# Half of the weights' low parts in a float32 block: a GpSimd subtraction or a transfer that adds

## The chip, the cores and the metric

The kernel runs on one core of a Trainium2 chip, as one launch. The metric is the device time of one execution in microseconds; the figure for a kernel is the median of several executions. Inputs and outputs lie in HBM.

## The reference, cut to what matters

One layer of a hybrid encoder block for 512 tokens and 1024 channels: a shared norm and input projection, an RWKV-7 branch (8 heads of 64) and a chunked Gated DeltaNet branch (4 heads of 128, chunks of 64), a gated merge, an output projection, then an MLP with a causal convolution.

```python
u = rms_norm(x, norm1_g[l])
p = u @ w_in[l]
p_rwkv, qkv, z, a_raw, b_raw, gate_a, gate_b = _split(p, IN_SPLITS)
y_a = rwkv7_mix(p_rwkv, ...) @ rwkv_proj[l]
y_b = gated_deltanet_mix(qkv, z, a_raw, b_raw, ...) @ gdn_proj[l]
mixed = jax.nn.sigmoid(gate_a) * y_a + jax.nn.sigmoid(gate_b) * y_b
x = x + mixed @ w_out[l]
h = causal_depthwise_conv(rms_norm(x, norm2_g[l]) @ ffn_up[l], ffn_conv_w[l])
h_gate, h_up = _split(h, (FFN_HIDDEN, FFN_HIDDEN))
x = x + (jax.nn.silu(h_gate) * h_up) @ ffn_down[l]
```

All of it is float32.

## The kernel before, in words

**Engines.** TensorE (PE) does the matmuls, VectorE (DVE), ScalarE (ACT) and GpSimd (POOL) the rest; SyncE (SP) issues every transfer. Each engine works through its own queue in order.

**Dense products.** A float32 weight is used as a sum of two parts of a format that PE takes at full rate: `hi`, the weight rounded to that format, and `lo`, what is left. An activation is likewise kept as `uh` and `ul`. A product of 128 output channels and 512 tokens is then three kinds of matmul over eight blocks of 128 input channels: lo·uh, hi·uh and hi·ul, 24 in all. `unit` (line 164 on) loads one such weight tile of 128x1024 (512 KB) into `raw` by one transfer on SP, and `halves_of` (line 153) makes `hi` and `lo` for each of its two halves of 128x512: ACT copies to `hi` (line 158), and a subtraction raw − hi gives `lo` (line 160). The subtraction goes by turns to GpSimd (the first half of a unit) and to VectorE (the second half): `POOL = "13"` and the running count modulo 4. `mm3` (line 185 issues its matmuls) uses the first half's `lo` in its first matmul. There are two `raw` buffers and four each of `hi` and `lo` (`HB = 4`), so half n+4 can be written only when PE is through with half n; buffers rotate in the order in which the units are called for.

**Stages.** `first_tiles` (to about 37 us) loads the activations and makes the first units. `mixing` then runs a list of steps, `ORDER`: `R` prepares a pair of RWKV heads (three units), `G` a DeltaNet head (three units), `g` a gate and `z` a DeltaNet gate (one unit each); `i` and `c` are the triangular inverses and the chunk recurrence of RWKV, `I` and `C` those of the DeltaNet heads. After `mixing` come the two branch projections, the merge, and the MLP.

**What sets the order.** The program is written step by step, and a scheduler lays the instructions of all steps into the engines' queues by its own estimates and by priorities: `unit` raises the priority of the load and of the halves, the chunk recurrences run beside the units of later steps. So while DVE works through an inverse, units of the next heads pass through ACT, GpSimd and PE.

**Lines that are spoken of.** `base_inverse` (lines 549 to 571) inverts 32x32 triangles on DVE alone: per row one multiplication into `invN` (line 565) and one addition into `invY` (line 567), each with two inputs in SBUF, one waiting for the other. `rwkv_prep` has DVE operations with two SBUF inputs at lines 496, 510, 512 and 515, `gdn_chain` at line 937; `split` makes `uh` and `ul` at lines 203 and 204. On GpSimd there are also a few small operations: the MEMSETs of lines 557, 641 and 642, the copies of lines 559, 807 and 818, a power of 128x4 elements at line 798.

Of the kernel before, what the change touches and what calls it, by code (L numbers as in the profile page):

```python
# [9 lines left out]
F32 = mybir.dt.float32  # L10
F32R = mybir.dt.float32r
BF16 = mybir.dt.bfloat16
AF = mybir.ActivationFunctionType
ALU = mybir.AluOpType
# [6 lines left out]
POOL = "13"  # L21
# [2 lines left out]
TAGS = {"T": 4, "P": 3, "T2": 2}  # L24
BANKS = {"D": 2, "A": 3, "B": 3}
ORDER = "R0 g0 R1 g1 g2 g3 a i0 G0 G1 z1 c0 z0 g4 g5 R2 I0 R3 C0 g6 i1 c1 g7 g8 G2 G3 g9 z3 g10 z2 g11 I1 g12 C1 g13"
RAWG = 1

BLK = 4
# [67 lines left out]
class Body:  # L97
    def __init__(self, tc, a, o, ctx):
        self.tc, self.nc, self.a, self.o, self.ctx = tc, tc.nc, a, o, ctx
        self.uid = 0  # L100
        self.halves = 0
        self.second = False
        self.spilled = {}

# [46 lines left out]
        self.second = False  # L151


    def halves_of(self, raw, o, w=512):
        nc = self.nc
        hi = self.stream.tile([128, 512], F32R, tag="hi", name=self.nm("hi"), bufs=HB)
        lo = self.stream.tile([128, 512], F32R, tag="lo", name=self.nm("lo"), bufs=HB)
        nc.scalar.activation(hi[:, 0:w], raw[:, o:o + w], AF.Copy)  # L158
        self.halves += 1
        self.on(str(self.halves % 4)).tensor_tensor(out=lo[:, 0:w], in0=raw[:, o:o + w], in1=hi[:, 0:w].bitcast(F32),  # L160
                                                    op=ALU.subtract)
        return hi, lo, w // 128

    def unit(self, src, n=1024, ahead=True):
        nc = self.nc
        parts = []
        with self.tc.high_priority() if ahead else nullcontext():
            raw = self.stream.tile([128, 1024], F32, tag="raw", name=self.nm("raw"), bufs=2)
            nc.sync.dma_start(out=raw[:, 0:n], in_=src)
            for o in range(0, n, 512):  # L170
                parts.append(self.halves_of(raw, o, min(512, n - o)))
        return parts


# [87 lines left out]
    def first_tiles(self, xp):  # L262
# [68 lines left out]
        for i, (m, out) in enumerate(((4, first[1]), (0, first[2]), (8, first[0][:, 8, :]))):  # L331
            self.shifted(m, out, self.dense_in(m, act, "A", after if m == 4 else None), r)
            for k in UN[i]:
# [3 lines left out]
                self.split(self.uh[:, k, :], self.ul[:, k, :], un)  # L337
        for i in range(RAWG):
            self.gate(i, act=act, rstd=r)
# [38 lines left out]
    def mixing(self, first):  # L378
        nc = self.nc
        self.wc = self.mp.tile([128, 4, 8], F32, name="wc")  # L380
        self.rs2 = self.mp.tile([128, 4, 8], F32, name="rs2")
        R, G = {}, {}
        first = {0: first}

        def chain(g):
            self.rwkv_chain(g, R)
            self.rwkv_out((2 * g, 2 * g + 1), R)

        def inverse(g):
            self.gdn_inverse(g, G)  # L390

        for step in ORDER.split():
            op, i = step[0], int(step[1:] or 0)
            if op == "g" and i in self.spilled:
                continue
            if op == "R":
                R[i] = self.rwkv_prep(i, first.get(i))
            elif op == "a":
                self.gdn_gates()
            elif op == "G":  # L400
                G[i] = self.gdn_prep(i)
            elif op == "z":
                self.gdn_z(i)
            elif op == "g":
                self.gate(i)
            else:
                with self.stream2():
                    dict(i=lambda g: self.rwkv_inverse(g, R), c=chain, I=inverse, C=lambda g: self.gdn_chain(g, G))[op](i)
        self.gates = [self.rp.tile([128, 9, T], F32, tag="R", name=self.nm("R")) for _ in range(2)]
        for i in range(16):  # L410
            if i in self.spilled:
                nc.sync.dma_start(out=self.gates[i % 2][:, i // 2, :], in_=self.spilled[i])
            else:
                self.gate(i, self.gates[i % 2][:, i // 2, :])


        y = [self.inv(x) for x in "NAY"]
        y = [t[:, o:o + T] for t in y[:2] for o in (0, T)] + [y[2], self.t("P")] + [self.work.tile([128, T], F32, tag="BK", name=self.nm("BK"), bufs=2) for _ in range(2)]
        y = [t.bitcast(F32R) for t in y]
        for i in range(4):  # L420
            self.split(y[i], y[4 + i], self.yf[:, i, :])
        self.project(0, lambda k: (y[k], y[4 + k]))
# [836 lines left out]
```

## Time and profile before

| | |
|---|---|
| runs | 890.07, 891.26, 891.31 us (median 891.26) |
| the profiled execution | 889.34 us, of which the span of its instructions is 887.6 us |
| busy in the span: PE, DVE, ACT, POOL | 854.3, 653.5, 466.0, 210.3 us (96, 74, 53, 24%) |
| the chain that ended last, by engine | PE 68%, DVE 16%, ACT 6%, issue 3%, POOL under 1% |
| line 160 on POOL | 124 recorded, 170.6 us, 1376 ns each |
| line 160 on DVE | 124, 88.2 us, 711 ns each |
| line 158 on ACT | 248, 152.7 us, 619 ns each |
| TensorE clock granted | 0.997 of full speed |
| transfers | 84.25 MB, 29.6% of the time of the 16 DMA engines |

The busy time of an engine says how long it was at work, not whether anybody waited for it; a matmul's end is modelled and PE's instructions overlap, so PE is busy in the record also while it is not streaming. The chain is followed back from the last instruction: at each step to what released it, or to the instruction before it on its engine. It is the view that says where time would be saved, stage by stage, and it changes as soon as one of its links does.

### The profile page before, as it was taken

The page shows a single profiled execution, that of the slowest core. Times are in us where ns is not written, and L with a number is a line of the kernel's source. Part 1 is how long each engine was busy: PE and PEld are TensorE (multiplying, and loading weights), DVE is VectorE, ACT ScalarE, POOL GpSimd, SP SyncE. Part 2 cuts the span into 40 slices and gives each one's busy share as a digit, 9 for nine tenths or more (in the row PEclk, how much of TensorE's full clock was granted, in tenths as well). Part 3 has the DMA queues.
Part 4 walks back from the last instruction along what each step waited for, and adds up shares of the span by engine and source line. Part 5 has one row for each costly group of instructions (what it writes and reads, how often), then busy time and mean ns, then how long its engine had stood idle before and what let it go on. Part 6 is the DMA issues. An engine that isn't in the chain of part 4 may idle for free.

```text
span 887.6 us, 13504 instructions
## 1 busy us (share of the span) xinstructions
PE 854.3 (96%) x5046; PEld 679.3 (77%) x5046; DVE 653.5 (74%) x1247; ACT 466.0 (53%) x905; POOL 210.3 (24%) x189
## 2 busy tenths in 40 slices
PE   8989999999999899999999999999999999999996
PEld 4867677766777677668788878888888888898895
DVE  6899897973899978944577448998866666573665
ACT  7745357666543677573544455554444444443333
POOL 2231123111111221111122212223222222342431
PEclk9999999999999999999999999999999999999998
DMA  7321222212112211136153223332323332332333
GB/s 265 115 89 59 73 71 73 69 57 68 48 60 72 71 50 60 60 109 213 49 194 113 95 72 95 96 95 98 116 95 95 95 96 89 111 104 82 104 87 132
DMA packets 29746, 84.25 MB, mean 95 GB/s; under 512 B 3312, under 2 KB 5488, under 8 KB 29680
## 3 DMA queue, kind: packets, MB, share of 16 engines
q1 hardware_dynamic: 29680, 83.39, 29.6%
q8 instruction: 40, 0.66, 0.3%
q14 instruction: 26, 0.21, 0.1%
HBM read 77.61 MB, written 5.77 MB: 94 GB/s over the span
## 4 chain that ended last, share of the span: by engine, by line
PE 68%; DVE 16%; ACT 6%; issue 3%; POOL 0%; DVEq 0%; ACTq 0%; POOLq 0%
PE D L185 43%; PE D L1089 5%; PE A L1089 4%; PE B L1089 3%; PE B L185 2%; DVE invN L565 2%; PE A L185 2%; DVE invY L567 2%; DVE P L771 1%; DVE lo L160 1%; DVE R L531 1%; DVE BK L510 1%; DVE BK L515 1%; ACT hi L158 1%; PE B L663 1%
## 5 line engine op out<-in xcount | busy, mean ns | idle before, releaser
L160 POOL TENSOR_TENSOR lo<-raw,hi 128x512 fp32r<-128x512 f32 x124 | 170.6, 1376 | 578.4 <-ACT hi L158 577.2
L158 ACT ACTIVATE hi<-raw 128x512 fp32r<-128x512 f32 x248 | 152.7, 619 | 181.4 <-PE D L185 87.2
L185 PE MATMUL D<-uh,lo 128*128 128x512 f32 x384 | 160.5, 418 | 2.7 <-DVE R L375 1.4
L185 PE MATMUL D<-uh,hi 128*128 128x512 f32 x384 | 151.4, 395 | 0.0
L185 PE MATMUL D<-u2h,lo 128*128 128x512 f32 x352 | 137.9, 392 | 0.0
L185 PE MATMUL D<-u2h,hi 128*128 128x512 f32 x352 | 137.8, 392 | 0.0
L160 DVE TENSOR_TENSOR lo<-raw,hi 128x512 fp32r<-128x512 f32 x124 | 88.2, 711 | 46.3 <-ACT hi L158 45.7
L185 PE MATMUL D<-ul,hi 128*128 128x512 f32 x384 | 109.1, 406 | 0.0
L185 PE MATMUL D<-u2l,hi 128*128 128x512 f32 x352 | 95.1, 392 | 0.0
L185 PEld LDWEIGHTS D<-uh,lo 128*128 128x128 f32 x384 | 72.2, 188 | 21.3 <-issue 3.1
L1006 DVE SCALAR_TENSOR_TENSOR P<-T,vecs,P 128x511 f32<-128x511 f32 x88 | 81.8, 929 | 6.9 <-ACT P L1004 2.6
L185 PEld LDWEIGHTS D<-uh,hi 128*128 128x128 f32 x384 | 72.3, 188 | 14.6 <-issue 1.0
L185 PEld LDWEIGHTS D<-ul,hi 128*128 128x128 f32 x384 | 69.3, 188 | 16.3 <-issue 1.0
L185 PEld LDWEIGHTS D<-u2h,hi 128*128 128x128 f32 x352 | 66.1, 188 | 14.9 <-issue 0.2
L185 PEld LDWEIGHTS D<-u2h,lo 128*128 128x128 f32 x352 | 66.1, 188 | 14.7 <-issue 0.2
L185 PEld LDWEIGHTS D<-u2l,hi 128*128 128x128 f32 x352 | 66.1, 188 | 14.1
L1003 DVE TENSOR_TENSOR T<-D,acc 128x512 f32<-128x512 f32 x44 | 30.2, 686 | 32.0 <-PE D L185 28.2
L565 DVE TENSOR_TENSOR invN<-invA,invY 128x60 f32<-128x60 f32 (+24 forms) x124 | 39.6, 319 | 3.0
L1004 ACT ACTIVATE P<-T,vecs 128x512 f32<-128x512 f32 x44 | 31.7, 721 | 16.5 <-DVE T L1003 14.5
L567 DVE TENSOR_TENSOR invY<-invY,invN 128x60 f32<-128x60 f32 (+24 forms) x124 | 32.3, 260 | 3.0
L771 DVE SCALAR_TENSOR_TENSOR P<-D,vecs,P 128x511 f32<-128x511 f32 (+2 forms) x36 | 26.7, 742 | 0.8 <-ACT P L769 0.7
L1195 ACT ACTIVATE P<-P 128x512 f32<-128x512 f32 x22 | 13.7, 624 | 21.0 <-DVE P L1006 21.0
(437 smaller groups left out, 1556.5 us busy)
## 6 DMA issues: line engine op xcount, KB each, us to landing
raw<-w_in SPq DMA_DIRECT2D x44, 512.0 KB, 3.6
raw<-ffn_up SPq DMA_DIRECT2D x44, 512.0 KB, 3.5
raw<-ffn_down SPq DMA_DIRECT2D x9, 512.0 KB, 3.5
raw<-w_out SPq DMA_DIRECT2D x8, 512.0 KB, 3.5
raw<-ffn_down SPq DMA_DIRECT2D x16, 256.0 KB, 2.9
spill<-T SPq DMA_DIRECT2D x14, 256.0 KB, 2.0
R<-spill SPq DMA_DIRECT2D x14, 256.0 KB, 3.9
raw<-ffn_down SPq DMA_DIRECT2D x9, 384.0 KB, 3.1
```

The costliest lines, as they stand in the source:

```text
L158: nc.scalar.activation(hi[:, 0:w], raw[:, o:o + w], AF.Copy)
L160: self.on(str(self.halves % 4)).tensor_tensor(out=lo[:, 0:w], in0=raw[:, o:o + w], in1=hi[:, 0:w].bitcast(F32), op=ALU.subtract)
L185: nc.tensor.matmul(ps, t[:, w[k]], x[k][p], start=(first and i == 0 and q == 0), stop=(last and i == len(parts) - 1 and q == len(seq) - 1))
L510: nc.vector.scalar_tensor_tensor(out=bkh[h][s, :, sb, :], in0=q(K, s, h), scalar=self.hkk[s, hp:hp + 1], in1=q(at, s, h), op0=ALU.mult, op ...
L565: nc.vector.tensor_tensor(out=w, in0=rows[:, t, 0:t].unsqueeze(2).broadcast_to([128, t, n]), in1=Ym[:, t, c:G].unsqueeze(1).broadcast_to([ ...
L567: nc.vector.tensor_tensor(out=Ym[:, 0:t, c:G], in0=Ym[:, 0:t, c:G], in1=w, op=ALU.add)
L771: nc.vector.scalar_tensor_tensor(out=cv[:, sh:], in0=ps[:, 0:T - sh], scalar=w(3 - sh), in1=cv[:, sh:], op0=ALU.mult, op1=ALU.add)
L1003: nc.vector.tensor_tensor(out=h, in0=ps, in1=self.acc2, op=ALU.mult)
L1004: nc.scalar.activation(cv, h, AF.Copy, scale=w(2))
L1006: nc.vector.scalar_tensor_tensor(out=cv[:, sh:], in0=h[:, 0:T - sh], scalar=w(2 - sh), in1=cv[:, sh:], op0=ALU.mult, op1=ALU.add)
L1089: nc.tensor.matmul(out, w, x, start=bank not in started, stop=stop)
L1195: nc.scalar.activation(g, g, AF.Silu)
```

## The change

`halves_of` gets the source of the load as an argument. In the steps of `ORDER` up to `G3` (the fourth DeltaNet head), where GpSimd would subtract, ACT instead writes −hi into `lo` (line 165 of the changed kernel), and GpSimd issues a transfer that reads the same 256 KB of the weight from HBM once more and adds them onto `lo` in SBUF (line 166). These are 31 halves: R1, g1, g2, g3, G0, G1, z1, z0, g4, g5, R2, R3, g6, g7, g8, G2 and G3. `first_tiles`, the steps after `G3` (g9 to g13, z3, z2), the projections and the MLP keep the subtraction, and so do all halves of VectorE.

```diff
+ACCLAST = "G3"
...
-    def halves_of(self, raw, o, w=512):
+    def halves_of(self, raw, o, w=512, src=None):
         nc = self.nc
         hi = self.stream.tile([128, 512], F32R, tag="hi", name=self.nm("hi"), bufs=HB)
         lo = self.stream.tile([128, 512], F32R, tag="lo", name=self.nm("lo"), bufs=HB)
         nc.scalar.activation(hi[:, 0:w], raw[:, o:o + w], AF.Copy)
         self.halves += 1
+        if src is not None and self.accumulate and str(self.halves % 4) in POOL:
+            nc.scalar.activation(lo[:, 0:w], hi[:, 0:w].bitcast(F32), AF.Copy, scale=-1.0)
+            nc.gpsimd.dma_start(out=lo[:, 0:w], in_=src[:, o:o + w], accum_op=ALU.add)
+            return hi, lo, w // 128
         self.on(str(self.halves % 4)).tensor_tensor(out=lo[:, 0:w], in0=raw[:, o:o + w], in1=hi[:, 0:w].bitcast(F32),
                                                     op=ALU.subtract)
         return hi, lo, w // 128
...
-                parts.append(self.halves_of(raw, o, min(512, n - o)))
+                parts.append(self.halves_of(raw, o, min(512, n - o), src))
...
-        for step in ORDER.split():
+        for n, step in enumerate(ORDER.split()):
             op, i = step[0], int(step[1:] or 0)
+            self.accumulate = n <= ORDER.split().index(ACCLAST)
```

The scheduler lays the queues out anew. Lines of the changed kernel are 8 or 9 higher than before (160 is 168, 158 is 162, 185 is 193, 905 is 914).

ScalarE in G0, the first DeltaNet head: `hi` and `lo` are the halves of its units, `T` and `P` the convolution's tiles. Before:

```order
L158 ACTIVATE hi_1304<-raw_1302 128x512
L774 ACT_TABLE_LOAD
L774 ACTIVATE T_1149<-P_1144 128x512
L769 ACTIVATE P_1188<-D_1163,vecs 128x512
L158 ACTIVATE hi_1308<-raw_1302 128x512
```

The same place in the changed kernel:

```order
L162 ACTIVATE hi_1313<-raw_1311 128x512
L165 ACTIVATE lo_1314<-hi_1313 128x512
L783 ACT_TABLE_LOAD
L783 ACTIVATE T_1156<-P_1151 128x512
L778 ACTIVATE P_1196<-D_1171,vecs 128x512
L162 ACTIVATE hi_1318<-raw_1311 128x512
```

The negative copy stands behind its `hi`, ahead of the work of the head.

GpSimd a little later, in G0 and G1 (`kn` is the key norm, `gs` the gates). Before:

```order
L807 COPY T_1256<-gs 128x512
L160 TENSOR_TENSOR lo_1409<-raw_1406,hi_1408 128x512
L798 TENSOR_TENSOR kn_1196<-kn_1196,mhalf 128x4
L818 COPY gegl<-T_1269 128x4
L160 TENSOR_TENSOR lo_1497<-raw_1494,hi_1496 128x512
```

In the changed kernel:

```order
L816 COPY T_1265<-gs 128x512
L807 TENSOR_TENSOR kn_1204<-kn_1204,mhalf 128x4
L166 DMA lo_1420<-w_in 128x512
L827 COPY gegl<-T_1278 128x4
L166 DMA lo_1509<-w_in 128x512
```

Each subtraction has become the issue of a transfer in the same place; once, as here, it has changed places with a small operation.

TensorE where the recurrence of the first two DeltaNet heads (`B`) begins between the halves of R3 (`D`). Before:

```order
L905 MATMUL B_2597<-G_1108 128x128
L185 MATMUL D_2699<-uh,lo_2692 128x512
L185 MATMUL D_2699<-uh,hi_2691 128x512
L185 MATMUL D_2699<-uh,lo_2692 128x512
L185 MATMUL D_2699<-uh,hi_2691 128x512
L909 MATMUL B_2597<-vn_2599,G_1108 128x128
L912 MATMUL B_2595<-G_1108,vn_2599 128x128
L185 MATMUL D_2699<-uh,lo_2692 128x512
```

In the changed kernel:

```order
L914 MATMUL B_2619<-G_1114 128x128
L193 MATMUL D_2722<-uh,lo_2714 128x512
L193 MATMUL D_2722<-uh,hi_2713 128x512
L193 MATMUL D_2722<-uh,lo_2714 128x512
L193 MATMUL D_2722<-uh,hi_2713 128x512
L193 MATMUL D_2722<-uh,lo_2714 128x512
L193 MATMUL D_2722<-uh,hi_2713 128x512
L193 MATMUL D_2722<-uh,lo_2714 128x512
L193 MATMUL D_2722<-uh,hi_2713 128x512
L193 MATMUL D_2722<-ul,hi_2713 128x512 x4
L918 MATMUL B_2619<-vn_2621,G_1114 128x128
L921 MATMUL B_2617<-G_1114,vn_2621 128x128
```

The recurrence steps move behind the dense work by up to one half (12 matmuls) here; further on other steps move ahead of it by as much. From the projections on, PE's order is the same.

## Rows read from the trace of the kernel before

**Rows 1.** Busy time of each engine in three stretches (us from the start).

```profile
core 0: us, PE busy (x) PEld busy (x) DVE busy (x) ACT busy (x) POOL busy (x), PEclk, DMA share, GB/s
37.00:350.00 313.00, 295.47 (x2126) 223.07 (x2126) 263.94 (x626) 184.92 (x418) 61.60 (x75) 1.00 0.21 69
...
250.00:300.00 50.00, 47.10 (x249) 36.09 (x248) 47.24 (x112) 22.02 (x37) 7.31 (x6) 1.00 0.22 69
...
425.00:888.00 463.00, 453.27 (x2178) 378.17 (x2176) 317.08 (x447) 211.65 (x352) 128.00 (x92) 0.99 0.33 101
```

**Rows 2.** The chain of waits, 37 to 350 us: shares by line.

```profile
by line: PE D L185 18.9%; issue 6.4%; DVE invN L565 6.0%; DVE invY L567 5.2%; DVE P L771 3.3%; DVE lo L160 2.8%; DVE R L531 2.5%; DVE BK L510 2.1%; DVE BK L515 2.0%; ACT hi L158 1.7%; DVE R L496 1.3%; DVE P L512 1.2%; PE B L663 1.2%; ACT R 
```

**Rows 3.** Timeline around 102 us: start, length, instruction, idle time before it.

```profile
102.25 0.22 DVE L567 TENSOR_TENSOR invY<-invY,invN 128x58 f32<-128x58 f32 x1
102.48 1.29 POOL L160 TENSOR_TENSOR lo<-raw,hi 128x512 fp32r<-128x512 f32 x1 [8.43 <-ACT hi L158]
102.50 1.34 DVE L565 TENSOR_TENSOR invN<-invA,invY 128x56 f32<-128x56 f32 x1
```

**Rows 4.** Pieces of the chain of waits in order of time: start, length, what.

```profile
63.96 1.72 DVE P L512
85.08 1.43 DVE BK L510
102.50 1.35 DVE invN L565
...
253.12 1.70 DVE R L496
262.23 1.39 DVE BK L515
...
292.18 1.28 DVE invY L567
...
301.38 1.27 POOL lo L160
```

**Rows 5.** Lines of DVE, 37 to 350 us: count, shortest/median/longest in ns.

```profile
L565 DVE TENSOR_TENSOR invN<-invA,invY x93: 161/241/1342, 101.1 to 315.5; 128x126 f32<-128x126 f32 x6, 128x30 f32<-128x30 f32 x5, 128x56 f32<-128x56 f32 x4, 128x78 f32<-128x78 f32 x4
...
L512 DVE TENSOR_TENSOR P<-P,T x4: 679/688/1706, 64.0 to 261.1; 128x512 f32<-128x512 f32 x4
...
L510 DVE SCALAR_TENSOR_TENSOR BK<-P,sp,T x16: 468/484/1428, 61.9 to 260.3; 64x256 f32<-64x256 f32 x16
...
L496 DVE TENSOR_TENSOR R<-P,Ep x8: 673/682/1776, 56.9 to 255.5; 64x512 f32<-64x512 f32 x8
...
L515 DVE TENSOR_TENSOR BK<-P,T x16: 409/420/1376, 65.7 to 264.1; 64x256 f32<-64x256 f32 x16
...
L160 DVE TENSOR_TENSOR lo<-raw,hi x35: 670/681/1187, 38.6 to 345.1; 128x512 fp32r<-128x512 f32 x35
```

**Rows 6.** Timeline around 47 us: GpSimd writes, DVE works beside it.

```profile
46.63 0.53 POOL L557 MEMSET invY<- 128x512 f32 x1 [1.23 <-DVE T L335]
47.09 0.68 DVE L160 TENSOR_TENSOR lo<-raw,hi 128x512 fp32r<-128x512 f32 x1
47.10 0.20 POOL L641 MEMSET SUV<- 64x128 f32 x1
```

**Rows 7.** Groups by line and form, 37 to 350 us: busy, mean ns, idle before.

```profile
L158 ACT ACTIVATE hi<-raw 128x512 fp32r<-128x512 f32 x69 | 43.2, 626 | 26.8 <-issue 10.9 <-PE D L185 9.3 <-POOL kn L798 4.7
...
L160 POOL TENSOR_TENSOR lo<-raw,hi 128x512 fp32r<-128x512 f32 x34 | 46.6, 1372 | 178.3 <-ACT hi L158 178.3
```

**Rows 8.** Timeline at the first unit of R1.

```profile
37.93 0.64 ACT L158 ACTIVATE hi<-raw 128x512 fp32r<-128x512 f32 x1 [0.49 <-DMA raw<-w_in]
...
44.56 0.40 PE L185 MATMUL D<-uh,lo 128*128 128x512 f32 x1
...
44.80 0.39 PE L185 MATMUL D<-uh,hi 128*128 128x512 f32 x1
```

**Rows 9.** Issues of transfers, whole span: KB each, median us from issue to landing.

```profile
raw<-ffn_down SPq DMA_DIRECT2D x16, 256.0 KB, 2.9
...
raw<-w_in SPq DMA_DIRECT2D x4, 256.0 KB, 5.6
```

More of the change, by code (lines that the diff above doesn't have):

```diff
@@ L101, in __init__ @@
         self.halves = 0
+        self.accumulate = False
         self.second = False
```

## The prediction

> **What bounds the kernel now.** I read the busy times by stretch first. After 425 us PE is at work for 98% of the time, and the change touches nothing there; from 37 to 350 us, the steps in which the 31 halves lie, DVE is busy for 264 of 313 us, in one stretch for 47.2 of 50 [rows 1]. The chain of waits over the same 313 us says who is waited for: PE's dense matmuls hold 18.9% of it, but two lines of the inverse, 565 and 567, hold 11.2% together, and seven more DVE lines are named [rows 2]. So this part is a chain through DVE, with dense matmuls as filling; what DVE saves on the chain ends the stage earlier, and what follows moves with it.
>
> Then the timeline. At 102.48 us GpSimd begins a subtraction of 1.29 us. At 102.50 DVE begins one of its small multiplications and needs 1.34 us for it, until the subtraction ends; the instruction before it, of nearly the same size, took 0.22 [rows 3]. Both read two operands from SBUF. The lines of DVE show the pattern: medians of 0.24 to 0.69 us, the longest ones about 1 us above them [rows 5]. GpSimd is off the chain, yet it stops the engine that is on it.
>
> **What the change removes.** 31 of GpSimd's subtractions, 1.37 us each [rows 7], 42.5 us of an idle engine and worth nothing by themselves. What counts is the stalls of DVE on the chain. I count the pieces of the chain that coincide with one of the 31 subtractions. Eight are of the inverse, from 1.35 us at 102.50 to 1.28 at 292.18 [rows 4], together 9.5 us; eight ordinary ones would be 8 x 0.24 = 1.9 [rows 5], so 7.6 us go. Four are of the head preparation: 1.72 − 0.69 at 63.96, 1.43 − 0.48 at 85.08, 1.70 − 0.68 at 253.12, 1.39 − 0.42 at 262.23 [rows 4, 5], together 4.0 us. One piece is a subtraction itself, 1.27 us at 301.38, where the chain runs through GpSimd and DVE at once [rows 4]. Sum: 7.6 + 4.0 + 1.3 = **12.9 us**, at 13 places of 31.
>
> Not all of that comes back. Behind a DVE instruction that is freed of 1 us stands the next wait, most often for PE (busy 295 of 313 us by the record, if not always streaming [rows 1]) or for ACT. I take eight tenths, 10.3 us: the pieces lie mostly in stretches such as 250 to 300 us, where DVE has next to no idle time, and there a saving is a saving of throughput. The ends are 0 and 12.9 us. Beyond that, the other 18 subtractions may have stalled DVE off the chain; were six of them worth as much as the one at 102.50, 1.1 us, that would be 6.6 us more.
>
> **What it adds on ACT.** 31 copies from SBUF to SBUF of the form of line 158: 31 x 0.626 = 19.4 us [rows 7]. ACT is busy for 185 of 313 us [rows 1], so there is room, but its queue is in order. Of the copies that are there now, 43.2 us [rows 7], 1.7% of 313 = 5.3 us are on the chain [rows 2], 12%. I take the same share of the new ones: **2.4 us** lost. The ends: nothing (all in idle time), and 19.4 us (all on the chain).
>
> **What it adds on GpSimd and in the transfers.** No transfer issued by GpSimd, and none that adds, is in this trace. GpSimd's part is bounded by its shortest and longest work near by, 0.2 us for a MEMSET [rows 6] and 1.37 for the subtraction [rows 7]; its engine is idle for 80% of the stretch [rows 1], so I take no price for either. The landing is bounded by the loads of 256 KB from SP, 2.9 and 5.6 us [rows 9]. From `hi` to a finished `lo` it is then 0.63 + 0.2 + 2.9 = 3.7 to 0.63 + 1.37 + 5.6 = 7.6 us, where the subtraction needs about 1.4. The cover: with four buffers, three halves lie between the writing of a half and its use. 69 halves in 313 us [rows 7] are 4.5 us each, 13.6 us of cover; where PE does nothing but dense work, 12 matmuls at 0.24 us (44.56 to 44.80 [rows 8]) are 2.9 us, 8.6 for three. The only place below is the first of the 31: its `hi` ends at 38.57 and is used at 44.56 [rows 8], 6.0 us later, so up to 1.6 us late at the upper end. I take 5 us for the whole path, so **0**. The extra load, 31 x 256 KB = 8.1 MB over 313 us, is 26 GB/s beside 69, with the DMA engines 21% busy [rows 1]: 0.
>
> **What it moves.** GpSimd's other work waited behind subtractions that waited for ACT; it now waits behind issues that wait for ACT 0.63 us longer. That is the key norm, the gates' copies and the MEMSETs, which stand far ahead of their use or far behind. On PE the recurrence of the first two DeltaNet heads slips behind dense work by up to one half, 2.9 us, and later steps come earlier by about as much; both heads' ends stand where they stood. I take 0, with 2.9 us either way in the range.
>
> **The sum.** 10.3 − 2.4 = 7.9 us off the profiled execution's 889.34, so 881.4. The median of the runs shown, 891.26, lies 1.9 above that execution; for the median I therefore say **883.4 us**. About 0.2%, 1.8 us, is what a measurement of this kernel can tell from no change.
>
> **Rivals.**
>
> *The issue holds up DVE as the subtraction did.* If GpSimd, while it writes a transfer's descriptors, stops DVE's two-operand instructions for as long, nothing is gained and the copies on ACT are lost: 891.3 + 2.4 = 893.7 us; if it does so for half as long, some 889. Against it: at 47.09 us DVE subtracts two operands while GpSimd writes zeros at 46.63 and 47.10, and needs 0.68 us [rows 6], its median being 0.681 [rows 5]. So a GpSimd instruction that only writes is no obstacle in this trace. For it: no row shows an issue. Chance 0.15.
>
> *The transfer lands too late* (the slower side). PE's first matmul of each unit needs this `lo`, and PE's queue is in order, so everything behind it waits, the recurrences too. It decides from about 8.6 us between `hi` and landing, the cover at dense pace. Were it 12 us, a third of the 31 halves, those at the tightest pace, would be 3.4 us late each, 35 us; with half of that on the end's path, 883.4 + 17 = 901 us. Against it: 7.6 us is the most that the rows make likely, and 13.6 the usual cover. For it: an addition has to read its target as well, and GpSimd has to make the descriptors. The Trainium skill, page "SBUF — State Buffer", section "Specifications (TRN2)", speaks against this change at that point: descriptors of a transfer issued from GpSimd are written by GpSimd's cores, and these are locked out while VectorE runs an instruction that takes both ports; it gives 620 ns alone against about 3100 beside such a copy. By that, an estimate, a landing would be up to 2.5 us later, 10.1 us at the upper end, which is beyond the dense cover and short of the usual one. No row here shows such a wait. Chance 0.10.
>
> *Another chain takes over at once.* If beside the DVE chain one through PE and ACT is only a little shorter, the 10.3 us shrink to 3 or 4 and ACT's 2.4 eat most of it: 889 to 891 us. For it: ACT and issue waits have their own pieces in the chain [rows 2]. Against it: the DVE lines hold the more. Chance 0.15.
>
> **How the numbers follow.** The forecast, a gain of 4 to 13 us, or a few more where stalls off the chain count, has 0.60. Of the first rival's 0.15 I put 0.02 to faster, 0.07 to no change, 0.06 to slower; of the third's 0.15, 0.09 to faster, 0.05 to no change, 0.01 to slower; the second's 0.10 is slower. So faster 0.71, same 0.12, slower 0.17. The range: at the low end everything comes back and ACT's copies are free, 891.3 − 12.9 = 878.4, with the 6.6 us of the other stalls 871.8, so 872; at the high end the first rival, 894. The forecast's own range is 872 to 888. Left out are the late landing and a little below 872, together under 0.2.
>
> **What would show it.** Right: the medians of lines 565, 567, 512, 510, 496 and 515 stay, and their longest values between 37 and 350 us fall to the medians' neighbourhood, except beside the subtractions that are left; DVE's busy time there falls by 13 to 20 us; ACT's rises by 19; no dense matmul waits for `lo`; the last gate's work before the projections begins 8 us earlier. Wrong: DVE's long instructions are still there beside the issues (first rival); PE waits for a transfer into `lo` (second); DVE's busy time falls, but its idle time grows by as much (third).

## The result and the profile after

| | before | changed |
|---|---|---|
| median of the runs | 890.31 us (888.59 to 891.31, 7 runs) | 885.45 us (881.58 to 887.49, 7 runs) |
| the profiled execution, its span | 889.34, 887.6 us | 883.38, 881.6 us |
| TensorE clock granted | 0.997 | 0.993 |

The ratio is 0.9935, 95% interval [0.9918, 0.9952], which is 5.8 us; the medians lie 4.9 us apart. The forecast was 7.9. The runs of the changed kernel differ by more than those of before, and go with the granted clock: the two at 0.995 and 0.996 took 881.67 and 881.58 us, the three at 0.987 to 0.989 took 886.43 to 887.49.

The page's busy times first (before: PE 854.3, DVE 653.5, ACT 466.0, POOL 210.3):

```profile
PE 854.4 (97%) x5046; PEld 680.8 (77%) x5046; DVE 636.7 (72%) x1247; ACT 488.8 (55%) x940; POOL 195.6 (22%) x189
```

By stretch, the windows of [rows 1], the first cut at 345 us because the stage ends earlier:

```profile
core 0: us, PE busy (x) PEld busy (x) DVE busy (x) ACT busy (x) POOL busy (x), PEclk, DMA share, GB/s
37.00:345.00 308.00, 296.02 (x2113) 225.37 (x2112) 247.00 (x623) 204.23 (x447) 46.90 (x76) 0.99 0.39 96
250.00:300.00 50.00, 47.02 (x253) 36.71 (x252) 44.52 (x118) 28.68 (x46) 4.66 (x6) 0.99 0.42 101
425.00:881.00 456.00, 447.68 (x2149) 373.75 (x2148) 315.87 (x440) 210.26 (x350) 126.87 (x91) 0.99 0.32 102
```

DVE has lost 17 us of busy time in the whole, ACT gained 23. Between 250 and 300 us DVE is busy for 44.5 us instead of 47.2. After 425 us nothing is new.

The chain of waits over that stretch, to be held against [rows 2]:

```profile
by line: PE D L193 41.7%; issue 5.1%; DVE R L540 2.8%; DMA lo<-w_in 2.3%; DVE lo L168 2.1%; DVE BK L524 2.0%; DVE BK L519 2.0%; DVE P L780 2.0%; ACT R L616 1.9%; ACT hi L162 1.4%; PE B L684 1.2%; DMA raw<-w_in 1.1%; POOL kn L807 1.1%; PE B 
```

PE's dense matmuls have gone from 18.9% to 41.7%, and lines 565 and 567 (now 574 and 576), 11.2% before, are not among the names shown any more (the line is cut at the right). A new name is there, a transfer into `lo`, with 2.3%.

Why DVE left the chain is seen line by line, as in [rows 5] (count, shortest/median/longest in ns):

```profile
L574 DVE TENSOR_TENSOR invN<-invA,invY x93: 168/236/1017, 99.5 to 311.8; 128x126 f32<-128x126 f32 x6, 128x30 f32<-128x30 f32 x5, 128x56 f32<-128x56 f32 x4, 128x78 f32<-128x78 f32 x4
...
L576 DVE TENSOR_TENSOR invY<-invY,invN x93: 166/230/301, 99.7 to 312.0; 128x126 f32<-128x126 f32 x6, 128x30 f32<-128x30 f32 x5, 128x56 f32<-128x56 f32 x4, 128x78 f32<-128x78 f32 x4
...
L521 DVE TENSOR_TENSOR P<-P,T x4: 692/692/694, 64.4 to 256.4; 128x512 f32<-128x512 f32 x4
...
L519 DVE SCALAR_TENSOR_TENSOR BK<-P,sp,T x16: 468/480/486, 62.4 to 255.5; 64x256 f32<-64x256 f32 x16
...
L505 DVE TENSOR_TENSOR R<-P,Ep x8: 676/680/687, 57.7 to 250.6; 64x512 f32<-64x512 f32 x8
...
L524 DVE TENSOR_TENSOR BK<-P,T x16: 410/420/423, 65.2 to 258.4; 64x256 f32<-64x256 f32 x16
```

The medians are those of before. The longest have fallen from between 1.3 and 1.8 us to within two per cent of the median on lines 519, 521, 505 and 524, and to 0.30 us on line 576, whose widths differ. On line 574 the longest, at 310.41 us, stands beside a subtraction that was left. The timeline at the place of [rows 3] (start, length, instruction, idle time before it) shows GpSimd at an issue and DVE beside it at its usual pace:

```profile
101.88 0.88 POOL L166 DMA_DIRECT2D lo<-w_in  x1 [8.76 <-ACT lo L165]
101.98 0.24 DVE L574 TENSOR_TENSOR invN<-invA,invY 128x78 f32<-128x78 f32 x1
...
102.25 0.24 DVE L576 TENSOR_TENSOR invY<-invY,invN 128x78 f32<-128x78 f32 x1
```

The groups by line and form, 37 to 345 us, against [rows 7]:

```profile
L162 ACT ACTIVATE hi<-raw 128x512 fp32r<-128x512 f32 x69 | 43.3, 628 | 30.0 <-PE D L193 27.9 <-DMA raw<-w_in 1.8
L166 POOL DMA_DIRECT2D lo<-w_in x31 | 27.4, 884 | 183.9 <-ACT lo L165 127.0 <-ACT SUV L681 22.9 <-PE D L193 14.6
...
L165 ACT ACTIVATE lo<-hi 128x512 fp32r<-128x512 f32 x31 | 19.4, 626 | 0.6
...
L168 POOL TENSOR_TENSOR lo<-raw,hi 128x512 fp32r<-128x512 f32 x4 | 5.2, 1291 | 18.6 <-ACT hi L162 18.6
```

An issue holds GpSimd for 0.88 us, two thirds of the 1.37 of the subtraction. Of the VectorE instructions beside the 31 issues only two are much longer than usual, on line 784 at 117.96 us (1.89 us) and at 303.56 (1.65); beside both GpSimd also runs the copy of line 816, which reads SBUF.

**The loss.** The chain again, in order of time, at the first of the 31 halves:

```profile
37.75 0.64 ACT hi L162
...
38.42 0.63 ACT lo L165
...
39.68 6.97 DMA lo<-w_in
...
46.79 11.97 PE D L193 x44
```

The first transfer landed 6.97 us after its issue began. PE's timeline at the same place (in brackets the idle time and what ended it), the place of [rows 8]:

```profile
44.09 0.40 PE L473 MATMUL A<-xw,lora_l 128*128 128x512 f32 x1
46.79 0.77 PE L193 MATMUL D<-uh,lo 128*128 128x512 f32 x1 [2.30 <-DMA lo<-w_in]
47.35 0.63 PE L193 MATMUL D<-uh,hi 128*128 128x512 f32 x1
47.78 0.63 PE L193 MATMUL D<-uh,lo 128*128 128x512 f32 x1
```

PE waited 2.30 us for it (its first matmul comes 2.2 us later than the one at 44.56 us in [rows 8]), and the matmuls that follow start 0.43 us apart instead of the 0.24 of [rows 8]. The windows say why; the column after POOL is the granted clock:

```profile
46.60:50.00 3.40, 3.21 (x8) 2.57 (x9) 3.16 (x6) 0.63 (x1) 1.57 (x4) 0.50 0.91 204
50.00:54.00 4.00, 4.00 (x19) 3.22 (x18) 0.69 (x1) 2.67 (x5) 0.18 (x1) 1.00 0.12 43
299.20:302.60 3.40, 3.40 (x11) 2.72 (x10) 3.40 (x7) 2.72 (x10) 0.00 (x0) 0.50 0.46 110
```

For 3.4 us after that wait the granted clock is 0.50, the lower of its two levels (1.2 GHz), and a second such stretch follows a wait of PE of 2.60 us for DVE at 298.80. The first costs PE 8 x 0.2 = 1.6 us, an estimate from the spacing. The kernel before has no such stretch in the mixing.

The transfers also took more of the DMA engines than their bytes let expect. The queue of SP's loads and that of GpSimd's transfers (packets, MB, share of the 16 engines' span):

```profile
q1 hardware_dynamic: 29680, 83.39, 29.7%
q0 software_dynamic: 4464, 8.13, 5.8%
```

A MB that adds took 0.71% of the engines' span, a MB of the loads 0.36%.

### The profile page after: what moved, and what is told of

It reads as the page before. It is cut to its first block, busy times and chain, and to the rows that moved or that the text cites. A ratio compares the mean times of both kernels' runs of the same rounds, so it can differ in the third digit from the quotient of the medians.

```text
span 881.6 us, 13565 instructions
## 1 busy us (share of the span) xinstructions
PE 854.4 (97%) x5046; PEld 680.8 (77%) x5046; DVE 636.7 (72%) x1247; ACT 488.8 (55%) x940; POOL 195.6 (22%) x189
## 4 chain that ended last, share of the span: by engine, by line
PE 77%; DVE 11%; ACT 6%; issue 3%; DMA 2%; POOL 1%; SPq 0%; DVEq 0%; ACTq 0%; POOLq 0%
PE D L193 50%; PE D L1098 5%; PE A L1098 4%; PE B L1098 3%; PE A L193 3%; PE B L193 3%; DVE R L540 1%; DVE lo L168 1%; DMA raw<-w_in 1%; ACT hi L162 1%; DMA lo<-w_in 1%; DVE BK L524 1%; DVE BK L519 1%; DVE P L780 1%; ACT R L616 1%
## 5 line engine op out<-in xcount | busy, mean ns | idle before, releaser
L168 POOL TENSOR_TENSOR lo<-raw,hi 128x512 fp32r<-128x512 f32 x93 | 128.0, 1377 | 411.7 <-ACT hi L162 410.5
L193 PE MATMUL D<-uh,lo 128*128 128x512 f32 x384 | 163.1, 425 | 3.9 <-DMA lo<-w_in 2.3
L168 DVE TENSOR_TENSOR lo<-raw,hi 128x512 fp32r<-128x512 f32 x124 | 90.1, 726 | 44.5 <-ACT hi L162 43.8
L193 PEld LDWEIGHTS D<-uh,hi 128*128 128x128 f32 x384 | 73.1, 190 | 15.1 <-issue 1.4
L166 POOL DMA_DIRECT2D lo<-w_in x31 | 27.4, 884 | 183.9 <-ACT lo L165 127.0
L1013 ACT ACTIVATE P<-T,vecs 128x512 f32<-128x512 f32 x44 | 31.7, 721 | 17.0 <-DVE T L1012 15.1
L576 DVE TENSOR_TENSOR invY<-invY,invN 128x60 f32<-128x60 f32 (+24 forms) x124 | 30.1, 243 | 3.0
L574 DVE TENSOR_TENSOR invN<-invA,invY 128x60 f32<-128x60 f32 (+24 forms) x124 | 29.4, 237 | 3.0
```

Source lines behind the costliest of these rows:

```text
L166: nc.gpsimd.dma_start(out=lo[:, 0:w], in_=src[:, o:o + w], accum_op=ALU.add)
L193: nc.tensor.matmul(ps, t[:, w[k]], x[k][p], start=(first and i == 0 and q == 0), stop=(last and i == len(parts) - 1 and q == len(seq) - 1))
L574: nc.vector.tensor_tensor(out=w, in0=rows[:, t, 0:t].unsqueeze(2).broadcast_to([128, t, n]), in1=Ym[:, t, c:G].unsqueeze(1).broadcast_to([ ...
L576: nc.vector.tensor_tensor(out=Ym[:, 0:t, c:G], in0=Ym[:, 0:t, c:G], in1=w, op=ALU.add)
L1013: nc.scalar.activation(cv, h, AF.Copy, scale=w(2))
```

## The experiments

Edits are shown against the changed kernel. In e1, e2, e3 and e6 the scheduler's order is that of the changed kernel but for at most two instructions of PE, so that GpSimd's work alone differs. e2 leaves out the addition of the weight, e6 and e11 the subtraction, so these three do not compute the layer; the others do.

| run | median, us | before, us | ratio, 95% interval |
|---|---|---|---|
| e1 copy, GpSimd subtracts | 896.31 | 890.18 | 1.0066 [1.0054, 1.0079] |
| e2 no transfer | 878.59 | 890.18 | 0.9863 [0.9848, 0.9877] |
| e3 first one subtracts | 880.46 | 890.18 | 0.9892 [0.9877, 0.9908] |
| e4 flag left on | 888.80 | 890.18 | 0.9984 [0.9968, 1.0000] |
| e5 half copies, GpSimd subtracts | 890.32 | 889.55 | 1.0004 [0.9994, 1.0014] |
| e6 GpSimd reads one operand | 885.63 | 889.55 | 0.9954 [0.9940, 0.9967] |
| e7 e3 carried to g13 | 880.57 | 889.55 | 0.9899 [0.9883, 0.9916] |
| e8 VectorE subtracts | 890.03 | 889.55 | 0.9991 [0.9977, 1.0005] |
| e9 half copies twice | 893.05 | 890.24 | 1.0034 [1.0019, 1.0048] |
| e10 two copies and transfers | 881.90 | 890.24 | 0.9907 [0.9890, 0.9924] |
| e11 as e5, GpSimd writes zeros | 875.91 | 890.24 | 0.9834 [0.9815, 0.9852] |
| e12 VectorE's halves too | 875.93 | 889.35 | 0.9837 [0.9814, 0.9859] |

One thing blurs differences of a few us between these runs. In the last 4 to 7 us of the program every profiled execution is at granted clock 0.50. Most have further time at it before: none in the kernel before and e10, 3.4 us in e2, e3, e5 and e7, 6.8 in the changed kernel, e4, e6 and e12, 10.2 in e11, 13.6 in e1 and e9, 17.1 in e8. Those of e1:

```profile
51.70:55.10 3.40, 3.40 (x9) 2.66 (x8) 2.32 (x2) 1.38 (x4) 1.28 (x1) 0.50 0.21 77
246.30:253.10 6.80, 6.80 (x28) 5.79 (x27) 5.08 (x8) 0.73 (x2) 0.00 (x0) 0.50 0.00 0
314.50:317.90 3.40, 3.40 (x10) 2.66 (x9) 3.36 (x7) 3.05 (x13) 0.43 (x1) 0.50 0.49 135
```

Such time costs PE at most half of itself, so up to 6.8 us in e1 and 1.7 in e2, an estimate. How much of it lies in the executions without a profile, their mean clock tells only roughly.

### e1 and e2: the subtraction, or nothing, in the transfer's place

```diff
-            nc.gpsimd.dma_start(out=lo[:, 0:w], in_=src[:, o:o + w], accum_op=ALU.add)
+            nc.gpsimd.tensor_tensor(out=lo[:, 0:w], in0=raw[:, o:o + w], in1=hi[:, 0:w].bitcast(F32), op=ALU.subtract)
```

> The changed kernel with one thing undone: the 31 negative copies on ScalarE stay, but GpSimd then subtracts raw - hi into lo instead of issuing the transfer. The order of all instructions on VectorE, ScalarE and SyncE is that of the changed kernel, on TensorE two instructions differ. Theory (GpSimd's subtraction, reading two operands from SBUF, is what stops VectorE): the gain of 4.9 us goes, and the copies cost what they cost, so 890 to 893 us; the long ones of the inverse's line 574 are back at 1.3 us, VectorE is busy for 13 to 20 us more than in the changed kernel. Rival A (the new order that the scheduler laid out made the gain): 885 to 887 us, with the long instructions back. Rival B (the copies are dear, the 12 per cent of them on the chain was too little): over 895 us.

```diff
-            nc.gpsimd.dma_start(out=lo[:, 0:w], in_=src[:, o:o + w], accum_op=ALU.add)
+            nc.gpsimd.memset(lo[:, 0:4].bitcast(F32), 0.0)
```

> The changed kernel without the 31 transfers: GpSimd zeroes four columns of lo instead, so the addition of the weight is left out, and nothing of it is waited for. The order of the instructions is that of the changed kernel. It is what the change would give with transfers that cost nothing. Theory (the transfers cost only where the first of them lands late): the wait of 2.3 us at 46.8 us and the stretch at half clock behind it (some 1.6 us) go, so 3.9 us less than the changed kernel, 881 to 882 us, and the 0.9 us of each issue on GpSimd nowhere matter. Rival (issue or traffic, 0.42 to 0.46 of the DMA engines' time against 0.21 to 0.26, slow something all along): 875 to 879 us, with the milestones after 100 us running further and further ahead. If the wait at 46.8 is made up for later anyway: 885 us.

e1 took 896.31 us, slower than before and in the range of rival B, e2 878.59. That is below the 881 to 882 us of e2's theory and in the range of its rival. Between the two nothing differs but what GpSimd does in 31 places (and two instructions of PE), and that is 17.7 us; up to 5.1 of it may have come by way of the half clock. The timeline of e1 shows a pair:

```profile
103.88 1.29 POOL L166 TENSOR_TENSOR lo<-raw,hi 128x512 fp32r<-128x512 f32 x1 [8.47 <-ACT lo L165]
103.96 1.30 DVE L576 TENSOR_TENSOR invY<-invY,invN 128x81 f32<-128x81 f32 x1
```

So GpSimd's subtraction is what stopped VectorE, and rival A falls: with the new order and the subtractions the kernel is slower than before. But e1 lies 6.1 us above before, more than the 2.4 put down for the copies; e5 and e9 ask whether the copies or the order make it.

### e3: the first half subtracts as before

```diff
-            nc.gpsimd.dma_start(out=lo[:, 0:w], in_=src[:, o:o + w], accum_op=ALU.add)
+            nc.gpsimd.dma_start(out=lo[:, 0:w], in_=src[:, o:o + w], accum_op=ALU.add) if self.halves > 13 else nc.gpsimd.tensor_tensor(out=lo[:, 0:w], in0=raw[:, o:o + w], in1=hi[:, 0:w].bitcast(F32), op=ALU.subtract)
```

> The changed kernel with the first of the 31 halves (the first of R1) subtracted on GpSimd as before, its copy on ScalarE kept; one instruction differs. Theory (the first landing, 6.97 us after its issue with two loads of 512 KB beside it, costs 2.3 us of wait and some 1.6 us at half clock): no wait of TensorE for lo at 46.8, granted clock 1.0 there, 881 to 882.5 us. Rival (the wait only takes the place of a later one, since the recurrence and the inverse are what the end waits for): 884.5 to 886 us, the milestones 3.8 us earlier at R1's second half and level by G0.

880.46 us, a little below the theory's range: one instruction of 31 was worth 5.0 us of medians, 3.6 of profiled spans (881.6 and 878.0). The two runs of the changed kernel at the highest clock, 881.6 us, lie only some 1.2 us above e3's median; so what the first landing costs may differ from run to run. Around 47 us the granted clock is whole (the other stretch, now at 296 us, is still there):

```profile
46.60:50.00 3.40, 2.61 (x10) 1.48 (x9) 3.35 (x6) 2.49 (x5) 1.15 (x3) 1.00 0.84 211
```

The starts of the first matmul with the n-th half's `lo` (n counted from 0; 8 and 9 are R1's first unit) say where each kernel gains. Before in us, the others as the difference to it:

| n | before | changed | e1 | e2 | e3 |
|---|---|---|---|---|---|
| 6 | 38.6 | −0.2 | −0.3 | 0.4 | −1.0 |
| 9 | 47.4 | 3.8 | −0.3 | 0.3 | −1.0 |
| 15 | 76.2 | −0.5 | 0.2 | −3.1 | −3.9 |
| 30 | 138.6 | −2.9 | 1.6 | −6.3 | −6.3 |
| 42 | 195.3 | −5.7 | 0.9 | −9.1 | −9.1 |
| 60 | 287.6 | −8.0 | 6.3 | −11.3 | −11.4 |
| 93 | 441.6 | −6.1 | 8.7 | −10.0 | −9.8 |
| 200 | 737.3 | −6.0 | 8.7 | −9.9 | −9.6 |

The 3.8 us that the changed kernel is behind at n = 9, 2.2 of wait and 1.6 of slow matmuls, stay with it to the end, where it is 3.6 us behind e3: the chain has no slack to take them up. In the profiled executions e3 with its 30 transfers runs level with e2, which has none. The runs do not: e2's four took 877.83 to 879.43 us, e3's four 879.77 to 883.24, with medians 1.9 us apart. So 30 transfers that land in time cost between nothing and some 2 us, and the record does not show where. The later part of the gain (from −11.4 to −9.8) is lost by both alike; both have 3.4 us at half clock there, from 296 us on, which can account for it (1.7 us at most).

Was the first landing late because it was the first that GpSimd issued? In e3 the first one, at 44.30 us, landed after 3.88 us. Landings there, shortest/median/longest in us, and in the changed kernel:

```profile
DMA to landing us min/median/max: 3.6/3.9/5.4
```

```profile
DMA to landing us min/median/max: 3.5/3.9/7.0
```

What sets the late one apart is what runs beside it: loads of 512 KB from SP were issued 0.53 us before and 0.64 us after it, and while it ran the DMA engines were busy for 72% of the time, against 39% in the whole stretch. e4, with the same issues at the same place, has 7.61 us there. That the loads make it late was not tried by moving them.

### e4: the flag left on

```diff
-ACCLAST = "G3"
+ACCLAST = "g13"
```

> The change carried to the last step of the mixing: the seven halves of g9, z3, g10, z2, g11, g12 and g13 too. Theory: of the subtractions left between 303 and 345 us the chain runs through one of 1.27 us at 332.6 and past one stalled VectorE instruction at 310.5 (0.94 against 0.24), so 1 to 2 us less than the changed kernel, 883.5 to 884.5 us; the landings have room, since dense work is not waited for there. Rival (more traffic and more copies on ScalarE, on which the chain lies for several us between 315 and 332): 885.5 to 888 us.

The edit did more than its text says: the last step of the list leaves the flag set, so the later gates, the projections and the MLP got transfers too, 118 in all. The issues of the three largest groups (KB each, median us to landing) and the place that it cost:

```profile
lo<-ffn_up POOLq DMA_DIRECT2D x44, 256.0 KB, 3.9
lo<-w_in POOLq DMA_DIRECT2D x40, 256.0 KB, 3.9
...
lo<-ffn_down POOLq DMA_DIRECT2D x18, 256.0 KB, 4.3
```

```profile
865.18 0.74 PE L1098 MATMUL B<-ah,lo 128*128 128x256 f32 x4 [2.26 <-DMA lo<-ffn_down]
```

888.80 us, above both ranges that were expected and 3.4 us worse than the changed kernel, with which it shares the late first landing. At 737 us its matmuls are 6.7 us ahead of before, where the changed kernel's are 6.0; in the last 30 us PE waits for transfers into `lo`, 2.26 us here, and the chain runs through two of them, 4.7 and 4.2 us. This is the second rival of the prediction, at a place where no other work covers the landing.

### e5 and e9: copies without the new order

```diff
-            nc.scalar.activation(lo[:, 0:w], hi[:, 0:w].bitcast(F32), AF.Copy, scale=-1.0)
+            nc.scalar.activation(lo[:, 0:256], hi[:, 0:256].bitcast(F32), AF.Copy, scale=-1.0)
```

and GpSimd's subtraction as in e1; e9 makes this copy twice.

> As e1 (copy on ScalarE, then GpSimd subtracts), but the copies write 256 of the 512 columns. With the shorter copies the scheduler lays out nearly the order of the kernel before (20 of 2998 rows of TensorE differ, 14 of 1178 of VectorE). It tells what made e1 slower by 6.1 us than before, the copies or the order that the scheduler made for them. Theory (copies: each holds up hi's successors in ScalarE's queue and GpSimd's subtraction behind it): six tenths of 6.1, so 893 to 894.5 us. Rival (the order): 889.5 to 891 us.

> e5 with each copy of 256 columns made twice, one after the other: 31 x 2 x 0.417 = 25.9 us of ScalarE, more than the 19.6 us of e1's copies, in nearly the order of the kernel before (30 of 2998 rows of TensorE differ, of e1 over 600). Theory after e5 (the order laid out for the copies, not their time on ScalarE, made e1 slower by 6.1 us): 889.5 to 891.5 us. Rival (the copies' time, once it passes some 13 us, is no longer covered): 896 us or more.

The copies of e5 and of e9 (shortest/median/longest in ns):

```profile
L165 ACT ACTIVATE lo<-hi x31: 400/417/449, 39.4 to 307.4; 128x256 fp32r<-128x256 f32 x31
```

```profile
L165 ACT ACTIVATE lo<-hi x62: 398/417/446, 39.8 to 312.5; 128x256 fp32r<-128x256 f32 x62
```

12.9 us of copies cost nothing that can be told (ratio 1.0004), as the rival of e5 said; 25.9 us cost 2.8 us, between e9's two theories. The 19.6 us of the changed kernel would by these two be worth some 1.7 us, an estimate on the line between them; the other 4 of e1's 6.1 us were not isolated by a run. They may be the scheduler's order in company with the stalls, and by e1's trace they may as well be the half clock: 5.4 us of what e1 is behind arise between n = 42 and n = 60, where 6.8 us of it lie.

### e11: the old order without the reads

```diff
-            nc.gpsimd.tensor_tensor(out=lo[:, 0:w], in0=raw[:, o:o + w], in1=hi[:, 0:w].bitcast(F32), op=ALU.subtract)
+            nc.gpsimd.memset(lo[:, 0:w].bitcast(F32), 0.0)
```

(against e5)

> e5 with GpSimd writing zeros to lo instead of subtracting (the subtraction is left out): nearly the order of the kernel before, and no reading by GpSimd in the 31 halves. With e5 it gives what these 31 subtractions cost in the old order, as e1 and e2 give it in the new one (17.7 us). Theory A (the order and the stops are separate prices): 872 to 874 us. Theory B (the new order only costs while GpSimd stops VectorE): as e2, 878 to 879.5 us, so 11 to 12 us for the 31 in the old order, against 12.9 counted from the chain.

GpSimd's writes and DVE's line 574:

```profile
L166 POOL MEMSET lo<- x31: 524/526/532, 38.2 to 291.8; 128x512 f32 x31
```

```profile
L574 DVE TENSOR_TENSOR invN<-invA,invY x101: 164/228/301, 95.4 to 344.7; 128x30 f32<-128x30 f32 x6, 128x126 f32<-128x126 f32 x6, 128x31 f32<-128x31 f32 x4, 128x56 f32<-128x56 f32 x4
```

875.91 us, 14.4 less than e5, between the two theories; e11's 10.2 us at half clock leave both open. GpSimd works for 0.53 us in the same 31 places, but it only writes, and line 574 has no long one left.

### e6: GpSimd reads one operand

```diff
-            nc.gpsimd.dma_start(out=lo[:, 0:w], in_=src[:, o:o + w], accum_op=ALU.add)
+            nc.gpsimd.tensor_copy(lo[:, 0:w], raw[:, o:o + w])
```

> The order of e1 and e2, with GpSimd copying raw to lo, one operand read from SBUF, in place of the subtraction that reads two (the subtraction is left out). Theory in its narrow form (only an instruction of GpSimd that reads two operands stops VectorE): near e2, 878.5 to 881 us, the longest of line 574 near its median of 0.23 us. Theory in its wide form (any reading of SBUF by GpSimd stops it, for as long as it lasts): the copy lasts about 0.6 us against 1.3 for the subtraction, so about half of the 17.7 us between e1 and e2 come back, 886 to 889 us, with long ones of 0.7 to 1 us.

885.63 us, just under the wide form's range and far above the narrow one's: 7.0 of the 17.7 us between e2 and e1. The timeline:

```profile
163.30 0.23 DVE L576 TENSOR_TENSOR invY<-invY,invN 128x69 f32<-128x69 f32 x1
...
163.39 0.61 POOL L166 CAST lo<-raw 128x512 fp32r<-128x512 f32 x1 [6.57 <-ACT lo L165]
163.56 0.52 DVE L574 TENSOR_TENSOR invN<-invA,invY 128x66 f32<-128x66 f32 x1
```

The multiplication before takes 0.23 us, this one 0.52, and it ends 0.08 us after GpSimd's copy. So GpSimd need not read two operands: one is enough to stop a two-operand instruction of DVE until the reading ends. The Trainium skill, page "SBUF — State Buffer", section "SBUF: two separate sides", states just that: a VectorE instruction with two SBUF inputs is blocked, for the whole of the other, by a GpSimd operation that reads SBUF and started first. These runs agree with 1.30 us beside the subtraction, 0.52 beside the copy and no effect of a MEMSET.

### e7, e8 and e10: other places, another engine, another order

e7 is e3 with `ACCLAST = "g13"` and the flag cleared after the last step.

> e3 with the seven halves of g9 to g13, z3 and z2 added, and no others (e4 left the flag set after the last step, so that there the projections and the MLP had transfers too). Theory (each subtraction left in the mixing still stops VectorE, and the end of the mixing is set by the last DeltaNet heads' recurrence on VectorE and TensorE): 1 to 2 us under e3, 878.5 to 879.5 us. Rival (seven more copies on ScalarE, which is on the chain there, cost as much): 880.5 to 883 us.

880.57 us, no difference from e3, in the rival's range: beyond G3 the seven transfers are worth nothing in the end. Whether the copies cost as much, as the rival had it, was not shown.

e8 drops copy and transfer, and the 31 subtractions run on VectorE:

```diff
-            nc.scalar.activation(lo[:, 0:w], hi[:, 0:w].bitcast(F32), AF.Copy, scale=-1.0)
-            nc.gpsimd.dma_start(out=lo[:, 0:w], in_=src[:, o:o + w], accum_op=ALU.add)
+            nc.vector.tensor_tensor(out=lo[:, 0:w], in0=raw[:, o:o + w], in1=hi[:, 0:w].bitcast(F32), op=ALU.subtract)
```

> The 31 subtractions moved to VectorE: no copies, no transfers, GpSimd free of them. VectorE gets 31 x 0.69 = 21 us of work more. Theory (what counts is VectorE's time, however it is lost): GpSimd's 31 subtractions cost 17.7 us between e1 and e2, 0.57 each, so VectorE doing them itself at 0.69 is worth about the same or a little worse: 888 to 894 us. Rival (a subtraction of VectorE's own can be laid into its idle time, a stop by GpSimd cannot): 880 to 886 us.

890.03 us, and DVE busy for 259 of 308 us as before (259.8 in the same window):

```profile
37.00:345.00 308.00, 298.03 (x2083) 227.40 (x2082) 259.23 (x644) 183.43 (x405) 19.96 (x44) 0.98 0.23 69
```

By the medians a subtraction on idle GpSimd costs as much as one that DVE does itself, and moving these 31 to GpSimd had bought nothing. A part of e8's time may be the half clock, 17.1 us in its profiled execution and so up to 8.5 us of PE's time; its three fastest runs, at clock 0.993, took 886.6 to 887.2 us.

e10 is e3 with the negative copy in two instructions of 256 columns, which brings the order near the old one.

> e3 with each negative copy written in two instructions of 256 columns, whereupon the scheduler lays out an order between that of the kernel before and that of the changed kernel, nearer to the former (118 of 2998 rows of TensorE differ from it, 379 of 3011 from the changed kernel); the copies take 25.9 us. Theory A (the changed kernel's order costs 6 us in any case): 874.5 to 877 us. Theory B (that order costs only while GpSimd's subtractions stop VectorE; with them gone it is as good as the old one): 879.5 to 882 us.

881.90 us, in theory B's range: once the stalls are gone, an order near the old one gains nothing over the new one (e10's longer copies are in it).

### e12: VectorE's halves too

```diff
-        if src is not None and self.accumulate and str(self.halves % 4) in POOL:
+        if src is not None and self.accumulate and self.halves > 13:
```

> e3 with VectorE's subtractions in the same steps replaced too: 61 transfers in all, 30 more copies on ScalarE (19 us, which then is busy for some 225 of 308 us), VectorE freed of another 21 us. Theory (VectorE's time bounds the mixing as before, priced by e8 against e11 at 14.1 us for 21.4 us of subtractions of its own): up to 14 us less than e3, less 3 to 6 us for the copies and the order, so 868 to 876 us. Rival (once 12 to 18 us of VectorE are saved, the dense matmuls and the copies on ScalarE are as long a chain, as the 41.7 per cent that the matmuls hold of the chain in the changed kernel suggest): 879 to 885 us; with transfers that come late under double traffic, over 885.

The window of 37 to 345 us, and the landings:

```profile
37.00:345.00 308.00, 298.84 (x2240) 226.96 (x2239) 231.72 (x603) 222.93 (x487) 74.36 (x106) 0.99 0.57 121
```

```profile
DMA to landing us min/median/max: 3.6/4.7/7.4
```

875.93 us, 13.4 under before and 4.5 under e3. DVE has 18 us less to do than in e3 (249.6), and a quarter of it comes back: PE is now busy for 299 of 308 us, and the chain names its dense matmuls with 38.8% and issue waits with 8.1%. Landings are 0.8 us later in the median under twice the traffic; PE waited for them twice, 1.9 us in all. Expected were 868 to 876 us by the theory, so it holds at its edge, and the rival's longer chain begins to show. Of the versions that leave nothing out it is the fastest, and beats both kernels. The half clock (6.8 us here, 3.4 in e3) is in this comparison too.

## Why the prediction was right, and where its sum was off

The sign and the range held. The forecast said 7.9 us of gain, the medians give 4.9, the profiled spans 6.0. The mechanism was right, but that the number came near is partly luck: the stalls were worth more than the sum had, and the landing, which it had at nothing, took a part of that back.

- **What bounds the mixing**: right. The lines of DVE lost their long instructions and left the chain, as said for lines 565, 567, 512, 510, 496 and 515; DVE's busy time fell by 17 us (13 to 20 were said), ACT's rose by 23 (19 were said; the copies themselves are 19.4). From 450 us on PE's dense work comes 6.0 us earlier; 8 were said for about that place.
- **The stalls, 12.9 us at 13 places, of which eight tenths**: too small. In nearly the old order the 31 subtractions cost 14.4 us (e5, e11), in the new one 17.7 (e1, e2), both give or take the half clock. A part is the count: the chain has nine pieces of the inverse beside the 31 subtractions, not eight, together 10.7 us, and runs through a second subtraction at 306.64, the last of the 31. By the prediction's own reckoning that makes 15.1 us at 15 places. The rest is the discount of two tenths, for which the runs show no need. The two that the count lacks (without the first, the inverse's pieces make the 9.5 us of the prediction):

```profile
126.01 1.23 DVE invN L565
...
306.64 1.28 POOL lo L160
```

- **ACT's copies, 2.4 us**: about right. e9 and e5 bracket it at 0.8 and 2.8 us over before for 12.9 and 25.9 us of copies; e2 lies 2.7 above e11, whose copies are half as wide and whose order is the old one (the intervals of the two ratios overlap).
- **The landing, 0**: this step failed. "The only place below is the first of the 31 ... up to 1.6 us late at the upper end. I take 5 us for the whole path, so 0." The path there was 8.3 us (37.75 + 0.64 to 46.65), beyond the upper end of 7.6 too. From the start of the issue to the landing it took 6.97 us, just what the upper end had for GpSimd's part and the landing together (1.37 + 5.6); what no term held is the 0.63 us between the end of the copy (38.42 + 0.63) and the start of the issue, 0.3 to 0.5 at the other 30. For the other 30 the path was 4.6 to 6.6 us, and they landed 3.0 us or more before PE's use: there 5 us was a good figure. The place was named rightly and its price set to nothing; and behind the wait came what no term held, the half clock.
- **Issue on GpSimd, traffic, PE's order, 0**: right to within some 2 us. e3 and e2 run level in the profiled executions and 1.9 us apart in the medians. The traffic was reckoned by its bytes, 26 GB/s beside 69 with the DMA engines 21% busy; their share rose to 39%, because these bytes take them about twice as long.
- **The first rival** is excluded by the issues' rows and by e3. The lockout of GpSimd's descriptor writing that the Trainium skill states (page "SBUF — State Buffer", section "SBUF: two separate sides", not the section that the prediction names) shows in no issue here: 31 of them, 860 to 1071 ns, beside a DVE that is busy for 247 of 308 us. Whether any instruction of the kind that it names stood beside them is not certain; the likeliest are two of line 476, with one SBUF input, 0.43 and 0.51 us long, and the issues beside them took 0.92 and 0.91 us. **The second rival** happened at one place of 31, in e4 at the end of the program too, and in e12 at two places (1.9 us). **The third** begins to show in e12; what limits e7 was not followed.

How the gain divides, by runs: −14.4 us (e5 to e11, the reads), +2.7 (e11 to e2, copies and order), +1.9 (e2 to e3, transfers in time), +5.0 (e3 to the change, the first landing). Each step begins where the one before it ends, so that the sum, −4.8, is the difference between the change and e5 and proves nothing. Each run's ratio to the kernel before in its own job gives −15.1, +2.6, +2.6 and +3.8 us instead; the single steps are sure to no more than 1 or 2 us.

## What to carry to other kernels

An engine that is off the chain can still hold the one that is on it: look for the same line's median and longest value far apart, and at what runs beside the longest. Where VectorE is the bound, give a long read on GpSimd to something that does not read SBUF through GpSimd, here a transfer; its price is the landing, so count the cover of each use one by one, the first and the last above all, and leave the uncovered ones as they were. Where a wait of TensorE is the price, count the slow matmuls behind it as well.

## What was not expected of the hardware

- Two waits of PE, 2.30 and 2.60 us, were each followed by 3.4 us at granted clock 0.50. The first one's true price was 3.8 us, not 2.2. The length of a wait does not tell by itself: the clock also fell within 1.4 us behind waits of 0.72 us (e6), 1.25 (e1) and 1.60 (e12), and the kernel before has waits of up to 1.8 us without it.
- The same transfer of 256 KB that adds took 3.5 to 5.1 us in 30 cases and 6.97 in one, with two loads of 512 KB issued within 0.7 us of it.
- A MB that adds took the DMA engines twice as long as a MB of plain loads (0.71 and 0.36% of their span).
- A copy on GpSimd that reads one operand stops DVE like a subtraction, for its own 0.61 us; a MEMSET of 0.53 us does not.
